# Two edits of a two-layer decoder: the order of the passes over the first layer's memory keys, and the chunk numbers at which the second layer's weight sums are made

## The chip, the cores and the metric

One Trainium2 chip, one core. The metric is the device time of one execution in microseconds (us), lower is better. The chip's engines run side by side, each through its own queue in order: TensorE (PE, matrix products; PEld is its loading of the stationary operand), VectorE (DVE), ScalarE (ACT), GpSimd (POOL) and SyncE (SP, which here only issues transfers).

## The reference, in short

A decoder trunk of two layers over 256 tokens of width 1024, in float32, with a memory of 256 rows that both layers attend to:

```
layer 0: x += short_conv_mixer(rms_norm(x)); x += mem_cross_attention(rms_norm(x), mem_n); x += swiglu(rms_norm(x))
shared keys and values (8 heads, partial rotary) from rms_norm(x), once
layer 1: x += moba_attention(rms_norm(x), shared k, v); x += mem_cross_attention(...); x += swiglu(...)
out = rms_norm(x)

short_conv_mixer: b, c, u = split(h @ w_in); (b * causal_conv3(c * u)) @ w_out
mem_cross_attention: k, v = split(mem_n @ w_kv); softmax(q k^T / 16) v, 4 heads; @ w_o
swiglu: g, u = split(h @ w_gu); (silu(g) * u) @ w_down, inner width 2816
```

There is one block of 256 keys, so layer 1's block-sparse attention is causal attention within it.

## The kernel before

**Chunks.** All weights come as 278 chunks of 128 x 1024 float32 (512 KB each), in the order in which they are used. SyncE loads them into one of 5 raw buffers. ScalarE rounds a chunk to its high part (`hi_`, a cast to fp32r), VectorE subtracts that from the raw chunk to have the low part (`lo_`). There are 10 such split pairs. Activations are split likewise. Each product is then three matmuls: high by high, high by low and low by high.

Chunks that matter here: 0 to 7 the first layer's memory keys (`memk0`), 8 to 31 the mixer's input matrices (`wc`, `wu`, `wb`), 72 to 135 layer 0's feed-forward, 160 to 167 the second layer's memory keys, 192 to 199 its memory output (`mo1`), 200 to 207 and on its feed-forward (`wr`, `wg`, `wu`, `wd`).

**Who sets the order.** A planner writes the whole program at build time. It keeps a clock for each engine with an estimated cost per instruction. Work beside the main line (norms, evictions, splits of chunks) are side jobs, which the planner asks after each matmul (`side.poll()`) whether they are due. So an edit in one loop can also change where other engines' instructions stand in their queues. Waits between engines are semaphores.

**The first layer's memory keys** (`mem_keys("memk0", ...)`, `scaled=False`). Eight column groups j of 128 in four accumulators (`acc_memk`, one bank of 2 x 256 each), over eight chunks k. Step (k, j) has three matmuls of 128 x 256: high by high and high by low (a = 0), then low by high (a = 1). For k = 0 to 3 the a = 0 matmuls of all j come first, then the low ones; for k = 4 and 5 the three stand together for each j; k = 6 and 7 are taken bank by bank, so that a bank is done early and can be evicted (`memk_u`).

While these run, side jobs prepare the mixer's input: `rows_factor` spreads the norm factor of x over the partitions by a matmul with a diagonal matrix (two pairs of `pb_x` matmuls, from `diag`), VectorE copies it (`x_rsb`) and multiplies with it (`mix_raw`, four pieces), ScalarE casts a product to its high part and VectorE subtracts for its low part (`mix`). The next products (`cu`) read `mix` and `wc`: the first one goes over k = 0 to 7 in eight matmuls of 128 x 512; its matmuls from k = 4 read the second chunk of `wc`, and those of k = 6 and 7 the last piece of `mix`.

**The weight sums.** Three pairs of feed-forward chunks (one in layer 0, two in layer 1: `jp` 4 and 8) are multiplied by seven products instead of eight, with sums of weight quarters T1 to T4 that are made in DRAM. `sum_steps(l, jp)` gives 16 steps in a fixed order, each a half: a copy issued by SyncE (L553) or an adding transfer issued by GpSimd (L551):

```
order = (("T1", "B11", False), ("T3", "B12", False), ("T1", "B12", True), ("T3", "B22", True),
         ("T2", "T1", False), ("T2", "B22", True), ("T4", "T2", False), ("T4", "B21", True))
```

A step is hung on a chunk number: `feed.hooks[n]` is run when chunk n is about to be loaded (`Feed.load_to`). `SUMS_AT` holds the first chunk and the end for each layer, between which its steps are spread evenly. Layer 0's 16 steps stand at 44 to 100. Layer 1's 32 steps stand at 128 to 217: those of `jp` 4 from 128 to 171, those of `jp` 8 from 174 to 217. The sums of `jp` 4 are first loaded from chunk 220 on, those of `jp` 8 from 250 on.

Of the kernel before, what the change touches and what calls it, by code (L numbers as in the profile page):

```python
# [21 lines left out]
KD = D // P  # L22
# [21 lines left out]
LATER = 2000  # L44
BANKWISE = 5
GROUPS = ((8,), (4, 8))
SUMS_AT = ((44, 104), (128, 220))


class Rows:  # L50
# [196 lines left out]
class Side:  # L247
# [15 lines left out]
    def step(self, item, last=0.0):  # L263
        if item[3]:
            return
        item[3] = True
        try:
            self.clock.last = last
            pause = next(item[1])
            item[0] = self.clock.last if pause is None else self.clock.now + pause  # L270
            item[4] = pause == 0
        except StopIteration:
            item[2] = True
            self.open.remove(item)
        item[3] = False
# [123 lines left out]
def yoco_kernel(  # L399
# [27 lines left out]
    def acc_tile(name):  # L427
        return ps_acc.tile([P, 512], F32, tag="acc", name=name)
# [11 lines left out]
    def held_half(name, shape=(P, 512)):  # L440
        return halves.tile(list(shape), F32, tag="half", name=name)
# [21 lines left out]
    def mm(o, l, r, start, stop, ns):  # L463
        nc.tensor.matmul(o, l, r, start=start, stop=stop)  # L464
        clock.note("pe", ns, [o], [l, r], 200)
# [69 lines left out]
    def sum_steps(l, jp):  # L535
        for name in ("T1", "T2", "T3", "T4"):
            for i in range(2):
                weight_sums[l, jp, name, i] = aside.tile([P, 2, 2 * T], F32, name=f"{name}_{l}_{jp}_{i}")

        def step(name, source, i, add):  # L540
            dst = weight_sums[l, jp, name, i]
            if source[0] == "T":
                src = weight_sums[l, jp, source, i]
            else:
                n = quarters[l, jp, source, i]
                src = chunks[n * P:(n + 1) * P].rearrange("p (a n) -> p a n", a=2)

            def run():
                clock.free["dma"] = max(clock.free["dma"], clock.now)
                if add:  # L550
                    nc.gpsimd.dma_start(dst, src, accum_op=OP.add, max_dma_last_dim=8192)  # L551
                else:
                    nc.sync.dma_start(dst, src)  # L553
                clock.note("dma", 3300 if add else 1460, [], [])

            return run

        order = (("T1", "B11", False), ("T3", "B12", False), ("T1", "B12", True), ("T3", "B22", True),
                 ("T2", "T1", False), ("T2", "B22", True), ("T4", "T2", False), ("T4", "B21", True))
        return [step(name, source, i, add) for name, source, add in order for i in range(2)]  # L560

    plan, _, quarters, ffn_steps = weight_plan()
    feed = side.feed = Feed(clock, plan, load_chunk, split_high, split_low)
# [107 lines left out]
    ones = const.tile([P, P], F32, name="ones")  # L671
# [162 lines left out]
    def mem_keys(name, mT, wait, scaled=True):  # L834
        kT = Act(side, [])
        accs = [acc_tile(f"acc_{name}_{b}") for b in range(4)]

        def bank_done(b):
            yield wait[b]
            u, j0 = kT.units[b // 2], 2 * (b % 2)  # L840
            if not scaled:
                acc = accs[b].rearrange("p (a t) -> p a t", a=2)
                scalar.copy(u[:, j0:j0 + 2, 0, :], acc)
                yield
                vector.tensor_sub(u[:, j0:j0 + 2, 1, :], acc, u[:, j0:j0 + 2, 0, :])
                return
            yield from side.hold("half")
            k_sb = held_half("k_sb", (P, 2, T))
            vector.tensor_mul(k_sb, accs[b].rearrange("p (a t) -> p a t", a=2),
                                 m_rsb[:, None, :].to_broadcast([P, 2, T]))  # L850
            yield
            scalar.copy(u[:, j0:j0 + 2, 0, :], k_sb)
            yield
            vector.tensor_sub(u[:, j0:j0 + 2, 1, :], k_sb, u[:, j0:j0 + 2, 0, :])
            side.give("half")

        def step(k, w, j, passes=((0, 0), (0, 1), (1, 0))):

            acc = accs[j // 2][:, (j % 2) * T:(j % 2 + 1) * T]
            mT.need(k)  # L860
            x = mT.parts(k)
            for a, b in passes:
                mm(acc, w[a][:, 0, j * P:(j + 1) * P], x[b], k == a == b == 0 and j % 2 == 0,
                   k == KD - 1 and a == 1 and j % 2 == 1, 0.4167 * T + 2)
                side.poll()

        for k in range(KD - 2):
            w = feed.take(f"{name}_{k}")
            if k == 0:
                for js in ((0, 1), (2, 3, 4, 5), (6, 7)):  # L870
                    for one in ((0, 0), (0, 1)):
                        for j in js:
                            step(k, w, j, (one,))
                for j in range(KD):
                    step(k, w, j, ((1, 0),))
                feed.free()
                continue
            if not scaled and k < 4:
                for ones in (((0, 0), (0, 1)), ((1, 0),)):
                    for j in range(KD):  # L880
                        step(k, w, j, ones)
                feed.free()
                continue
            for j in range(KD):
                if j == KD - 1:
                    feed.free()
                step(k, w, j)
        ws = [feed.take(f"{name}_{k}") for k in (KD - 2, KD - 1)]
        for b in range(4):
            for i in range(2):  # L890
                for j in (2 * b, 2 * b + 1):
                    step(KD - 2 + i, ws[i], j)
            if b % 2 == 0:
                kT.units.append(acts.tile([P, 4, 2, T], F32R, tag="unit", name=f"{name}_u{b // 2}"))
            kT.add_job(b % 2, b // 2, side.start(bank_done(b)))
        feed.free(2)
        return kT

    def mem_values(name, mT):
# [128 lines left out]
    feed.limit = len(plan)  # L1028
    feed.load_to(feed.lows + RAWS)
    memk0 = mem_keys("memk0", mT0, (1, 3000, 6000, 9000), False)  # L1030


# [6 lines left out]
        feed.hooks[36 + k] = [put_aside(k)]  # L1039

    for l in range(2):
        steps = [step for jp in GROUPS[l] for step in sum_steps(l, jp)]
        first, end = SUMS_AT[l]
        for n, step in enumerate(steps):
            feed.hooks.setdefault(first + (end - first) * n // len(steps), []).append(step)


    def short_conv(act, into):
# [506 lines left out]
    def moba(src, into):  # L1555
# [103 lines left out]
        proj_rows(act, "v1", keep_v)  # L1659
        mem_bank(1)  # L1660
        memk1 = mem_keys("memk1", mT1, (1, 1, 3000, 6000))
        side.finish(every)
        for job in attending.values():
# [96 lines left out]
```

## Time and profile before

| what | value |
|---|---|
| time, median of 3 runs | 784.99 us (784.41 to 785.51) |
| profiled execution: time, span | 784.93 us, 783.2 us |
| TensorE clock granted, mean | 0.998 |
| TensorE busy | 773.2 us (99%), 4147 matmuls |
| VectorE, ScalarE, GpSimd busy | 573.6, 458.9, 36.8 us |
| moved by DMA | 182.71 MB, 233 GB/s on average |

The span is the time between the first and the last recorded instruction; the execution's own time is 1.7 us longer. A line of a timeline gives start, length (us), engine, line, operation, what is written and read, and in brackets the idle time before it and what ended it. Matmuls overlap, so the distance between starts, not the length, is what one costs. Nearly all lines of ScalarE and VectorE carry L242 and those of TensorE L464, the helpers that record an operation, so lines are told apart by the names of their tiles.

### The profile page before, as it was taken

The numbers are of one execution on the slowest core, as the hardware profiler recorded it, in microseconds if no ns is written. First come the engines' busy times: TensorE is split into PE (matmuls) and PEld (weight loads), VectorE is DVE, ScalarE is ACT, GpSimd is POOL, SyncE is SP. The second block draws the span as 40 slices with busy tenths as digits, with TensorE's granted clock in tenths as the row PEclk, the third lists the DMA queues.
The fourth block names the chain that finished last, engine by engine and source line by source line (L and its number), as shares of the span: only waits on it lengthen the run. The fifth ranks groups of instructions, "written<-read, shape, count | busy, mean of one in ns | idle before, by whom it ended". The sixth has DMA issues, their size and how long they took to land.

```text
span 783.2 us, 11229 instructions
## 1 busy us (share of the span) xinstructions
PE 773.2 (99%) x4147; PEld 664.0 (85%) x4147; DVE 573.6 (73%) x872; ACT 458.9 (59%) x728; POOL 36.8 (5%) x68
## 2 busy tenths in 40 slices
PE   9999999999999999999999999999999999999996
PEld 8988888898888888888888889888988788888885
DVE  6988887768785666687766657877868776966874
ACT  6875665665654555566664573655756456655751
POOL 1000011000100000000110010030001000000000
PEclk9999999999999999999999999999999999999999
DMA  9776888916576755699787456899646746855931
GB/s 345 284 269 212 276 287 233 376 60 233 176 237 238 219 182 202 209 360 342 219 298 254 165 162 226 285 278 332 193 152 183 261 152 226 324 164 206 335 127 54
DMA packets 48807, 182.71 MB, mean 233 GB/s; under 512 B 6256, under 2 KB 7280, under 8 KB 46576
## 3 DMA queue, kind: packets, MB, share of 16 engines
q1 hardware_dynamic: 45968, 166.79, 59.5%
q0 software_dynamic: 2208, 14.68, 9.2%
q8 instruction: 32, 0.52, 0.3%
q10 hardware_dynamic: 576, 0.52, 0.2%
q14 instruction: 23, 0.19, 0.1%
HBM read 178.82 MB, written 28.31 MB: 264 GB/s over the span
## 4 chain that ended last, share of the span: by engine, by line
PE 93%; DVE 1%; DMA 1%; ACT 1%; issue 1%; POOLq 0%; DVEq 0%; ACTq 0%; SPq 0%
PE gu L464 17%; PE ff L464 14%; PE seven L464 7%; PE q_acc L464 6%; PE cu L464 6%; PE acc_mo L464 6%; PE acc_memv L464 6%; PE rows L464 4%; PE acc_memk L464 4%; PE pb L464 3%; PE acc_v L464 3%; PE acc_q L464 3%; PE acc_cout L464 3%; PE acc_o L464 3%; PE acc_k L464 3%; PE po L464 2%
## 5 line engine op out<-in xcount | busy, mean ns | idle before, releaser
L464 PE MATMUL ff<-hi_wd,guT 128*128 128x512 f32 (+1 forms) x352 | 108.3, 388 | 0.0
L464 PEld LDWEIGHTS ff<-hi_wd,guT 128*128 128x128 f32 x352 | 65.8, 188 | 12.8
L464 PE MATMUL ff<-lo_wd,guT 128*128 128x512 f32 (+1 forms) x176 | 68.3, 388 | 0.0
L242 DVE TENSOR_TENSOR gu_sb<-gu_sb,gu 128x256 f32<-128x256 f32 x48 | 20.0, 421 | 57.8 <-ACT gu_sb L242 56.9
L242 DVE TENSOR_TENSOR lo_wd<-raw_wd,hi_wd 128x1024 fp32r<-128x1024 f32 x44 | 53.5, 1221 | 7.4 <-ACT hi_wd L242 7.4
L242 ACT CAST hi_wd<-raw_wd 128x1024 fp32r<-128x1024 f32 x44 | 46.1, 1050 | 14.0 <-DMA raw_wd<-in_chunks_dram 13.0
L242 ACT COPY gu_sb<-gu 128x256 f32<-128x256 f32 x48 | 17.9, 372 | 62.1 <-PE gu L464 61.6
L464 PE MATMUL gu<-ffn,hi_wg 128*128 128x512 f32 x192 | 48.0, 390 | 0.0
L464 PE MATMUL gu<-ffn,hi_wu 128*128 128x512 f32 x192 | 47.6, 390 | 0.0
L464 PE MATMUL acc_memk<-mT,hi_memk 128*128 128x256 f32 x256 | 43.6, 287 | 0.1
L242 ACT CAST hi_wu<-raw_wu 128x1024 fp32r<-128x1024 f32 x32 | 33.5, 1051 | 15.3 <-DMA raw_wu<-in_chunks_dram 11.4
L464 PEld LDWEIGHTS gu<-ffn,hi_wg 128*128 128x128 f32 x192 | 35.9, 188 | 7.3
L464 PEld LDWEIGHTS gu<-ffn,hi_wu 128*128 128x128 f32 x192 | 35.8, 188 | 7.3
L464 PE MATMUL rows<-hi_wr,ffn 128*128 128x512 f32 x128 | 40.7, 395 | 0.0
L464 PE MATMUL acc_mo<-hi_mo,oT_mem 128*128 128x512 f32 x128 | 40.6, 393 | 0.0
L464 PE MATMUL acc_memv<-hi_memv,mT 128*128 128x512 f32 x128 | 39.6, 390 | 0.0
L242 DVE TENSOR_TENSOR lo_wu<-raw_wu,hi_wu 128x1024 fp32r<-128x1024 f32 x32 | 38.8, 1221 | 0.8 <-ACT hi_wu L242 0.5
L464 PEld LDWEIGHTS acc_memk<-mT,hi_memk 128*128 128x128 f32 x256 | 37.8, 193 | 0.8 <-ACT hi_memk L242 0.7
L464 PEld LDWEIGHTS ff<-lo_wd,guT 128*128 128x128 f32 x176 | 33.2, 188 | 6.3
L242 POOL TENSOR_TENSOR rs<-ms,neg_half 128x1 f32<-128x1 f32 x14 | 13.5, 964 | 469.1 <-DVE ms L242 459.8
L464 PE MATMUL q_acc<-mem,hi_mq 128*128 128x512 f32 x128 | 32.4, 394 | 0.0
L464 PE MATMUL acc_memk<-mT,lo_memk 128*128 128x256 f32 x128 | 31.2, 287 | 0.7 <-DVE lo_memk L242 0.5
(277 smaller groups left out, 1952.0 us busy)
## 6 DMA issues: line engine op xcount, KB each, us to landing
raw_wd<-in_chunks_dram SPq DMA_DIRECT2D x44, 512.0 KB, 5.3
raw_wu<-in_chunks_dram SPq DMA_DIRECT2D x32, 512.0 KB, 4.8
T<-in_chunks_dram POOLq DMA_DIRECT2D x24, 512.0 KB, 7.9
raw_wg<-in_chunks_dram SPq DMA_DIRECT2D x24, 512.0 KB, 5.1
raw_wT<-T SPq DMA_DIRECT2D x24, 512.0 KB, 4.9
raw_wB<-in_chunks_dram SPq DMA_DIRECT2D x18, 512.0 KB, 5.0
raw_memv<-in_chunks_dram SPq DMA_DIRECT2D x16, 512.0 KB, 5.4
raw_mq<-in_chunks_dram SPq DMA_DIRECT2D x16, 512.0 KB, 6.6
```

The costliest lines, as they stand in the source:

```text
L242: return call(out, *args, **kw)
L464: nc.tensor.matmul(o, l, r, start=start, stop=stop)
```

## The change

In `mem_keys` the unscaled case (only `memk0`) now takes chunks k = 0 to 6 with all a = 0 matmuls first and then the low ones; only k = 7 is taken bank by bank, with both column groups' a = 0 matmuls ahead of the low ones. The second layer's keys keep their order. `SUMS_AT` gets a range for each `jp`: layer 0 as before (44 to 100), layer 1's `jp` 4 at 108 to 153 and `jp` 8 at 157 to 202.

```diff
-SUMS_AT = ((44, 104), (128, 220))
+SUMS_AT = (((44, 104),), ((108, 157), (157, 206)))
...
-        for k in range(KD - 2):
+        whole = KD - 2 if scaled else KD - 1
+        for k in range(whole):
...
-            if not scaled and k < 4:
+            if not scaled:
                 for ones in (((0, 0), (0, 1)), ((1, 0),)):
                     for j in range(KD):
                         step(k, w, j, ones)
...
-        ws = [feed.take(f"{name}_{k}") for k in (KD - 2, KD - 1)]
+        ws = [feed.take(f"{name}_{k}") for k in range(whole, KD)]
         for b in range(4):
-            for i in range(2):
-                for j in (2 * b, 2 * b + 1):
-                    step(KD - 2 + i, ws[i], j)
+            for i, w in enumerate(ws):
+                for ones in (((0, 0), (0, 1), (1, 0)),) if scaled else (((0, 0), (0, 1)), ((1, 0),)):
+                    for j in (2 * b, 2 * b + 1):
+                        step(whole + i, w, j, ones)
...
-        feed.free(2)
+        feed.free(len(ws))
...
-        steps = [step for jp in GROUPS[l] for step in sum_steps(l, jp)]
-        first, end = SUMS_AT[l]
-        for n, step in enumerate(steps):
-            feed.hooks.setdefault(first + (end - first) * n // len(steps), []).append(step)
+        for jp, (first, end) in zip(GROUPS[l], SUMS_AT[l]):
+            steps = sum_steps(l, jp)
+            for n, step in enumerate(steps):
+                feed.hooks.setdefault(first + (end - first) * n // len(steps), []).append(step)
```

What this does to the queues, at three places. In the names, the numbers behind `memk0_` are the chunk k, and the last number is the tile's own. First TensorE's order around the second `pb_x` in the memory keys, before:

```order
L464 MATMUL acc_memk0_3_183<-mT0_1_109,hi_memk0_4_311 128x256 x2
L464 MATMUL acc_memk0_3_183<-mT0_1_109,lo_memk0_4_312 128x256
L464 MATMUL acc_memk0_0_180<-mT0_1_109,hi_memk0_5_342 128x256 x2
L464 MATMUL acc_memk0_0_180<-mT0_1_109,lo_memk0_5_343 128x256
L464 MATMUL acc_memk0_0_180<-mT0_1_109,hi_memk0_5_342 128x256 x2
L464 MATMUL pb_x_352<-diag_362,ones_102 128x128
L464 MATMUL acc_memk0_0_180<-mT0_1_109,lo_memk0_5_343 128x256
L464 MATMUL acc_memk0_1_181<-mT0_1_109,hi_memk0_5_342 128x256 x2
L464 MATMUL acc_memk0_1_181<-mT0_1_109,lo_memk0_5_343 128x256
```

and now:

```order
L464 MATMUL acc_memk0_3_183<-mT0_1_109,hi_memk0_5_352 128x256 x4
L464 MATMUL pb_x_366<-diag_367,ones_102 128x128
L464 MATMUL acc_memk0_0_180<-mT0_1_109,lo_memk0_5_353 128x256 x2
L464 MATMUL acc_memk0_1_181<-mT0_1_109,lo_memk0_5_353 128x256 x2
L464 MATMUL acc_memk0_2_182<-mT0_1_109,lo_memk0_5_353 128x256 x2
L464 MATMUL acc_memk0_3_183<-mT0_1_109,lo_memk0_5_353 128x256 x2
L464 MATMUL acc_memk0_0_180<-mT0_1_109,hi_memk0_6_371 128x256 x4
L464 MATMUL pb_x_366<-diag_395,ones_102 128x128
L464 MATMUL acc_memk0_1_181<-mT0_1_109,hi_memk0_6_371 128x256 x4
```

Before, the second `pb_x` stands behind the high matmuls of chunk 5's first bank and one low one; now it stands behind all of chunk 5 and the high matmuls of chunk 6's first bank.

Second, VectorE's order from right behind the copy of the norm factor (`x_rsb`) to the low parts of the mixer's first chunks (`wc`), before:

```order
L242 TENSOR_TENSOR mix0_raw_0_236<-mix0_raw_0_236,x_rsb_351 128x512
L242 TENSOR_TENSOR mix0_raw_1_238<-mix0_raw_1_238,x_rsb_351 128x512
L242 SCALAR_TENSOR_TENSOR lo_memk0_7_410<-raw_memk0_7_240,g_cols_106,hi_memk0_7_409 128x1024
L242 TENSOR_TENSOR mix0_0_278<-mix0_raw_0_236,mix0_0_278 128x2x256
L242 TENSOR_TENSOR mix0_raw_2_274<-mix0_raw_2_274,x_rsb_351 128x512
L242 TENSOR_TENSOR mix0_raw_3_276<-mix0_raw_3_276,x_rsb_351 128x512
L242 TENSOR_TENSOR mix0_0_278<-mix0_raw_1_238,mix0_0_278 128x2x256
L242 TENSOR_TENSOR memk0_u0_435<-acc_memk0_0_180,memk0_u0_435 128x2x256
L242 TENSOR_TENSOR mix0_1_279<-mix0_raw_2_274,mix0_1_279 128x2x256
L242 TENSOR_TENSOR mix0_1_279<-mix0_raw_3_276,mix0_1_279 128x2x256
L242 TENSOR_TENSOR lo_wc_0_0_462<-raw_wc_0_0_280,hi_wc_0_0_461 128x1024
L242 TENSOR_TENSOR lo_wc_0_1_475<-raw_wc_0_1_321,hi_wc_0_1_474 128x1024
```

and now:

```order
L242 TENSOR_TENSOR mix0_raw_0_236<-mix0_raw_0_236,x_rsb_365 128x512
L242 TENSOR_TENSOR mix0_raw_1_238<-mix0_raw_1_238,x_rsb_365 128x512
L242 SCALAR_TENSOR_TENSOR lo_memk0_7_412<-raw_memk0_7_240,g_cols_106,hi_memk0_7_411 128x1024
L242 TENSOR_TENSOR mix0_raw_2_274<-mix0_raw_2_274,x_rsb_365 128x512
L242 TENSOR_TENSOR mix0_0_278<-mix0_raw_0_236,mix0_0_278 128x2x256
L242 TENSOR_TENSOR mix0_raw_3_276<-mix0_raw_3_276,x_rsb_365 128x512
L242 TENSOR_TENSOR mix0_0_278<-mix0_raw_1_238,mix0_0_278 128x2x256
L242 TENSOR_TENSOR memk0_u0_454<-acc_memk0_0_180,memk0_u0_454 128x2x256
L242 TENSOR_TENSOR mix0_1_279<-mix0_raw_2_274,mix0_1_279 128x2x256
L242 TENSOR_TENSOR lo_wc_0_0_471<-raw_wc_0_0_280,hi_wc_0_0_470 128x1024
L242 TENSOR_TENSOR lo_wc_0_1_518<-raw_wc_0_1_321,hi_wc_0_1_517 128x1024
L242 TENSOR_TENSOR mix0_1_279<-mix0_raw_3_276,mix0_1_279 128x2x256
```

The low part of the last piece of `mix` (from `mix0_raw_3`) stood ahead of the two `lo_wc` subtractions and now stands behind them.

Third, GpSimd's queue from the second layer's last sums (the names end in layer, `jp` and half) to the norm factors (`rs`) of the second layer's feed-forward and of the output, before:

```order
L551 DMA T2_1_8_0_513<-in_chunks_dram 64x2048
L551 DMA T2_1_8_1_514<-in_chunks_dram 64x2048
L242 TENSOR_TENSOR rs_6030<-ms_6033,neg_half_100 128x1
L242 TENSOR_TENSOR rs_6093<-ms_6096,neg_half_100 128x1
L551 DMA T4_1_8_0_517<-in_chunks_dram 64x2048
L551 DMA T4_1_8_1_518<-in_chunks_dram 64x2048
L242 TENSOR_TENSOR rs_7627<-ms_7628,neg_half_100 128x1
L242 TENSOR_TENSOR rs_7716<-ms_7717,neg_half_100 128x1
```

and now:

```order
L551 DMA T2_1_8_0_503<-in_chunks_dram 64x2048
L551 DMA T2_1_8_1_504<-in_chunks_dram 64x2048
L551 DMA T4_1_8_0_507<-in_chunks_dram 64x2048
L551 DMA T4_1_8_1_508<-in_chunks_dram 64x2048
L242 TENSOR_TENSOR rs_6033<-ms_6036,neg_half_100 128x1
L242 TENSOR_TENSOR rs_6096<-ms_6099,neg_half_100 128x1
L242 TENSOR_TENSOR rs_7627<-ms_7628,neg_half_100 128x1
L242 TENSOR_TENSOR rs_7716<-ms_7717,neg_half_100 128x1
```

The two adds of T4 stood behind both factors of the feed-forward's norm and now stand ahead of them, right behind the adds of T2. On SyncE's queue their copies move likewise, from among the loads of `wg` and `wu` of the feed-forward to among those of `mo1`.

## Prediction

> **What bounds the kernel now.** I read the busy times first, then what TensorE waits for, then stretches of 10 us, and last the timelines of each engine around the waits.
>
> ```profile
> span 783.2 us, 11229 instructions
> PE 773.2 (99%) x4147; PEld 664.0 (85%) x4147; DVE 573.6 (73%) x872; ACT 458.9 (59%) x728; POOL 36.8 (5%) x68
> ```
>
> TensorE bounds it: it is busy for 773.2 of 783.2 us, so only 10.0 us are idle, and the change neither adds nor removes a matmul. All that it can win lies in those 10 us; all that it can lose is new idle time on TensorE. The waits of TensorE, longest first, say where they are:
>
> ```profile
> PE warm L464 <- DVE blank L763: 1.5, 1, 1.5
> PE pt_g L468 <- DVE gg L242: 1.3, 1, 1.3
> PE acc_memk L464 <- DVE lo_memk L242: 0.5, 1, 0.5
> PE acc_memk L464 <- DVE msp L242: 0.2, 1, 0.2
> ```
>
> The second lies in the last feed-forward block, the last two in the first layer's memory keys (`acc_memk`). The stretches show what else there is (time on each engine, clock, DMA share):
>
> ```profile
> 330.00:340.00 10.00, 10.00 (x46) 8.16 (x45) 8.35 (x9) 7.78 (x9) 0.00 (x0) 1.00 0.98 358
> 610.00:620.00 10.00, 8.71 (x41) 6.88 (x40) 6.48 (x9) 6.47 (x9) 0.00 (x0) 1.00 0.69 260
> 770.00:780.00 10.00, 6.90 (x48) 6.27 (x46) 7.17 (x23) 2.26 (x6) 1.46 (x2) 1.00 0.15 52
> ```
>
> The tail loses 3.10 us in this stretch alone, and neither edit touches it. The clock stays at 1.00. So the sum has two terms: the memory keys up to the gated convolution behind them, and the stretch at 612 us.
>
> **The edit of the memory keys.** TensorE's timeline:
>
> ```profile
> 1.46 2.95 PE L464 MATMUL warm<-blank 128*128 128x256 bf16 x13 [1.46 <-DVE blank L763]
> ...
> 10.88 2.08 PE L464 MATMUL acc_memk<-mT,hi_memk 128*128 128x256 f32 x16
> 12.80 1.12 PE L464 MATMUL acc_memk<-mT,lo_memk 128*128 128x256 f32 x8
> ...
> 16.64 0.40 PE L464 MATMUL acc_memk<-mT,hi_memk 128*128 128x256 f32 x2
> 17.21 0.39 PE L464 MATMUL acc_memk<-mT,lo_memk 128*128 128x256 f32 x1 [0.17 <-DVE msp L242]
> ...
> 20.76 0.38 PE L464 MATMUL pb_x<-diag,ones 128*128 128x128 f32 x2
> ...
> 24.86 0.39 PE L464 MATMUL acc_memk<-mT,lo_memk 128*128 128x256 f32 x1 [0.48 <-DVE lo_memk L242]
> ```
> ```profile
> 29.76 2.00 PE L464 MATMUL cu<-mix,hi_wc 128*128 128x512 f32 x8
> 31.60 1.98 PE L464 MATMUL cu<-mix,hi_wu 128*128 128x512 f32 x8
> ```
>
> Starts give the pitch: 16 high matmuls in 12.80 − 10.88 = 1.92, so 0.12 us each; 8 wide ones (`cu`) in 1.84, so 0.23 each. Chunks 4 to 7 took 29.76 − 16.64 = 13.12 us for 96 matmuls (11.52) and two pairs of `pb_x` (0.23 each, taking a pair to be like a wide matmul): 1.14 us are lost, and that is the most that this edit can win. It keeps chunk 4 from stopping for its low part, since 16 high matmuls (1.92 us) go first.
>
> But the edit also moves `pb_x`. The two pairs spread the norm factor of the first layer's input, which VectorE copies (`x_rsb`) before it multiplies anything of the mixer's input. The second pair stood behind four high matmuls and one low one of chunk 5 and now stands behind four high matmuls of chunk 6. From 16.64 chunk 4 takes 24 matmuls to 19.52, chunk 5's high ones last to 21.44, the first pair to 21.67, the low ones to 22.63, four of chunk 6 to 23.11. The second pair starts there, not at 20.76: 2.35 us later. VectorE's timeline of before:
>
> ```profile
> 21.80 0.42 DVE L242 COPY x_rsb<-pb_x 128x256 f32<-128x256 f32 x1
> 22.31 1.29 DVE L242 TENSOR_TENSOR mix_raw<-mix_raw,x_rsb 128x512 f32<-128x512 f32 x2
> 23.53 1.28 DVE L242 SCALAR_TENSOR_TENSOR lo_memk<-raw_memk,g_cols,hi_memk 128x1024 fp32r<-128x1024 f32 x1
> 24.72 0.68 DVE L242 TENSOR_TENSOR mix<-mix_raw,mix 128x512 fp32r<-128x512 f32 x1
> ...
> 27.73 1.28 DVE L242 TENSOR_TENSOR mix<-mix_raw,mix 128x512 fp32r<-128x512 f32 x2
> 28.93 2.36 DVE L242 TENSOR_TENSOR lo_wc<-raw_wc,hi_wc 128x1024 fp32r<-128x1024 f32 x2
> 31.20 0.68 DVE L242 TENSOR_TENSOR memk_u<-acc_memk,memk_u 128x512 fp32r<-128x512 f32 x1
> ```
>
> `x_rsb` started at 21.80, right behind the low part of chunk 6. Now it waits for the pair: 23.11 + 0.38 (that row's own length) and a semaphore's 0.1 (mix_raw at 22.31 began 0.09 behind the copy's end) is 23.6, which is 1.8 later. From there I add pitches of the rows: copy 0.51 → 24.1; two mix_raw products 1.22 → 25.3; chunk 7's low part 1.19 → 26.5; then, in the new order, mix_raw, mix, mix_raw, mix, `memk_u`, mix at 0.60 each → 30.1; two `lo_wc` 2.27 → 32.4. Only now comes the last mix part: 32.4 to 33.1. Before, it was done at 29.0, since it stood ahead of the two `lo_wc`.
>
> Who waits for it? The seventh matmul of the first `cu` product. On TensorE chunk 7's first low matmul waits for a low part that ends at 26.6 (high ones done at 26.2, so 0.4 lost), and the keys end at about 29.05, not 29.76. `cu` starts there. ScalarE, in its rows of before,
>
> ```profile
> 22.07 1.14 ACT L242 ACTIVATE hi_memk<-raw_memk,g_cols 128x1024 fp32r<-128x1024 f32 x1
> ...
> 26.22 1.14 ACT L242 CAST mix<-mix_raw 128x512 fp32r<-128x512 f32 x2
> 27.26 2.01 ACT L242 CAST hi_wc<-raw_wc 128x1024 fp32r<-128x1024 f32 x2
> ```
>
> ended the first `hi_wc` at 28.3. In the new order a mix cast stands ahead of each, and those wait for the late products: the two end at about 29.1 and 30.8. So the fifth matmul waits from 30.0 to 30.8, and the seventh from 31.3 to 33.1. Two matmuls later (0.46) the next product starts at 33.56 instead of 31.60: **+2.0 us**. Every later wait in this stretch had 0.9 us or more to spare in the order that I followed, and TensorE has no idle time behind it to take the delay up. Bounds: −1.1 (nothing late) and +2.6 (the casts and the 0.60 steps 10% longer).
>
> **The edit of the sums, at 612 us.** What the four engines and the queues did there, in time order:
>
> ```profile
> 590.52 0.56 POOL L242 TENSOR_TENSOR rs<-ms,neg_half 128x1 f32<-128x1 f32 x1 [38.44 <-DVE ms L242]
> ...
> 598.17 1.62 POOL L551 DMA_DIRECT2D T<-in_chunks_dram  x2
> ```
> ```profile
> 604.12 7.57 DMA raw_wd<-in_chunks_dram
> ```
> ```profile
> 610.56 1.05 ACT L242 CAST hi_wd<-raw_wd 128x1024 fp32r<-128x1024 f32 x1 [3.74 <-DMA raw_wd<-in_chunks_dram]
> 611.77 1.05 ACT L242 CAST hi_wd<-raw_wd 128x1024 fp32r<-128x1024 f32 x1 [0.16 <-DMA raw_wd<-in_chunks_dram]
> 612.72 0.38 ACT L242 ACTIVATE sg<-rows 128x256 f32<-128x256 f32 x1
> ```
> ```profile
> 611.94 0.39 PE L464 MATMUL rows<-hi_wr,ffn 128*128 128x512 f32 x1
> ```
> ```profile
> 613.61 0.44 PE pt_g L468 x2
> ```
> ```profile
> raw_wd<-in_chunks_dram SPq DMA_DIRECT2D x44, 512.0 KB, 5.3
> ```
>
> The last two adding transfers of the sums (T4 of pair 8) were issued at 598.17. Behind them `raw_wd` took 7.57 us against its median of 5.3. ScalarE waited 3.74 us for it, and behind its casts stood `sg`, from which `gg` and then the transpose `pt_g` come. TensorE was out of work at 611.94 + 0.23 = 612.17 and went on at 613.61: 1.44 us. In the new order these adds stand on GpSimd's queue ahead of the norm factor that ran at 590.52, so they are issued at least 13.5 us ahead of that load (604.12). With the median the last cast would end 2.3 us sooner, enough to cover 1.44: **−1.44 us**. Bounds: −1.44, and 0 if another transfer makes `raw_wd` late.
>
> **The other 31 steps.** Each of layer 1's 32 steps (half copies on SP's queue, half adds on GpSimd's) moves up by 14 to 20 chunks. On both queues they pass loads and norm factors and add no bytes. The earliest now fall into layer 0's own sum stage at 320 to 345 us, where the DMA share is already 0.98 for 10 us (above) and ScalarE's longest wait for a sum is
>
> ```profile
> 330.60 1.05 ACT L242 CAST hi_wT<-raw_wT 128x1024 fp32r<-128x1024 f32 x1 [1.76 <-DMA raw_wT<-T]
> ```
>
> TensorE is busy for all 10.00 us there, through that wait, so 1.76 us of delay is covered; what covers it are the split chunks waiting in the ten pairs. I cost these steps at 0, with +1.4 (a stop like that at 612) as the upper bound and −0.2 as the lower.
>
> **Sum.** 784.93 (the profiled execution, 0.06 below the median of 784.99; 1.7 of it lies around the span) + 2.0 − 1.44 + 0 = **785.5 us**. A measurement of this kernel can tell about 0.2% (1.6 us) from no change: the likeliest result is no change.
>
> **Rivals.** *Faster:* the factor comes late but costs nothing, since the last mix part was done 2.1 us before its matmul (29.0 against the seventh start, 29.76 + 6 × 0.23 = 31.14). Then 784.93 − 1.14 − 1.44 = 782.4. Against it: the delay of 1.8 alone would fit into 2.1, but the two `lo_wc` ahead of it take 2.27 more. It decides if the last mix part ends before 30.0. Halfway cases (net −0.4 in the keys) give 783.1 to 784.4.
>
> *Slower:* the moved transfers hold layer 0's sum stage. If the loads of T there land more than 2 to 4 us later than now, ScalarE's casts come so late that TensorE stops; priced like 612 us, at 1.4, this gives 786.9. For it: the share of 0.98; against it: no TensorE idle time for the same traffic in layer 1.
>
> *Clock:* the new pause of 1.8 us (31.3 to 33.1, with 0.8 shortly ahead of it) could cost TensorE its full clock. In the trace 1.3 us idle at 612 left the clock at 1.00. The 13 warm-up matmuls at the start took 2.95 us, 0.23 each against 0.12: such a stretch again is some +1.4, so 786.9. The Trainium skill ("TensorE: Matmul & The Clock Gate", Part 1: The HAM clock gate) has the clock halved after an idle window of about 3.4 us. By that rule a pause of 1.8 us should not do it; if it did, its window at half clock would cost an estimated 1.7 us. No run here shows a pause of that length in mid-kernel.
>
> **Chances.** Main case, 784.8 to 786.3: 0.5. Halfway: 0.12. Faster rival: 0.14. Slower rival: 0.2. Clock: 0.04. The range 782.3 to 787.1 takes in the single rivals and leaves out two stops together. Faster by over 0.2% (below 783.4) needs the keys to gain: 0.17 with the lower halfway cases; slower (above 786.6): 0.24; within: 0.59.
>
> **What would show it.** Right: `x_rsb` near 23.6; a wait of the seventh `cu` matmul on a mix part behind two `lo_wc`, second product at about 33.6; no wait of `pt_g` near 612; no new row in TensorE's waits between 320 and 400. Wrong: `cu` running through from 28.6, `raw_wd` still landing in 7 us, or waits on split chunks in layer 0's sums.

## The result, and the profile after

The changed kernel takes 792.13 us (median of 5 runs, 789.79 to 794.20) against 785.24 us (5 runs, 784.41 to 785.51): a ratio of 1.0088, with a 95% interval of 1.0067 to 1.0110. It is slower by 6.9 us, and the forecast of 785.5 us is wrong. The profiled execution has a span of 790.0 us, 6.8 more than that of before (783.2). Of all executions of the kernels below, one ran in a slower state (962.66 us at a mean granted clock of 0.752, of the new keys with pair 8 alone moved); it is in none of the ratios and counts.

TensorE's waits in the changed kernel (total us, times, longest):

```profile
PE pt_r L468 <- DVE r L242: 2.3, 1, 2.3
PE cu L464 <- DVE mix L242: 1.6, 1, 1.6
PE warm L464 <- DVE blank L763: 1.5, 1, 1.5
PE acc_memk L464 <- ACT hi_memk L242: 0.9, 1, 0.9
PE seven L464 <- DVE g L242: 0.8, 1, 0.8
PE ff L464 <- ACT guT L242: 0.7, 1, 0.7
PE gu L464 <- ACT hi_wu L242: 0.5, 1, 0.5
PE cu L464 <- ACT hi_wc L242: 0.3, 1, 0.3
PE acc_memk L464 <- DVE lo_memk L242: 0.2, 1, 0.2
```

The wait of `pt_g` is gone, the wait on `mix` is there as forecast, and four waits are new to which the forecast's sum gave no price: `seven`, `gu`, `ff` and `pt_r`. To see what each costs, I compared the times at which TensorE first uses each of the 278 chunks in the two traces. The difference moves only at these places: +0.8 at the start (the wait on `hi_memk`, before anything that differs), +2.0 at the keys, +0.3 near 55 us, +2.8 between 336 and 390 us, +2.2 ahead of the queries at 416 us, +0.1 later, −1.5 at 612 us. Before rounding these add up to 6.8.

**The keys went as forecast.** The changed kernel's TensorE and then VectorE in the first 35 us:

```profile
17.45 2.08 PE L464 MATMUL acc_memk<-mT,hi_memk 128*128 128x256 f32 x16
...
33.87 0.73 PE L464 MATMUL cu<-mix,hi_wc 128*128 128x512 f32 x2 [1.64 <-DVE mix L242]
34.44 1.99 PE L464 MATMUL cu<-mix,hi_wu 128*128 128x512 f32 x8
```
```profile
24.32 0.42 DVE L242 COPY x_rsb<-pb_x 128x256 f32<-128x256 f32 x1 [1.29 <-PE pb_x L464]
...
30.85 2.36 DVE L242 TENSOR_TENSOR lo_wc<-raw_wc,hi_wc 128x1024 fp32r<-128x1024 f32 x2
33.12 0.69 DVE L242 TENSOR_TENSOR mix<-mix_raw,mix 128x512 fp32r<-128x512 f32 x1
```

From chunk 4 to the second product it is 34.44 − 17.45 = 16.99 us, before 31.60 − 16.64 = 14.96: +2.03 for a forecast of +2.0. The norm factor is copied late, the last part of mix comes behind the two `lo_wc`, and the seventh matmul waits for it.

**So did the stop at 612 us.** The stretch that had 8.71 us of TensorE work before has no gap now:

```profile
610.00:620.00 10.00, 10.00 (x46) 8.20 (x45) 9.22 (x11) 5.78 (x8) 0.00 (x0) 1.00 0.71 228
```

ScalarE, which waited 3.74 us for the landing of `raw_wd` before, now waits for TensorE alone, and briefly:

```profile
615.40 1.05 ACT L242 CAST hi_wd<-raw_wd 128x1024 fp32r<-128x1024 f32 x1 [0.29 <-PE rows L464]
616.79 1.05 ACT L242 CAST hi_wd<-raw_wd 128x1024 fp32r<-128x1024 f32 x1 [0.33 <-PE rows L464]
```

**What the forecast missed** lies where pair 4's steps went. GpSimd's adds in the changed kernel, and the chain of waits behind them:

```profile
323.31 0.78 POOL L551 DMA_DIRECT2D T<-in_chunks_dram  x1 [11.48 <-DMA T<-in_chunks_dram]
328.07 0.78 POOL L551 DMA_DIRECT2D T<-in_chunks_dram  x1 [3.98 <-DMA T<-in_chunks_dram]
...
397.57 0.84 POOL L551 DMA_DIRECT2D T<-in_chunks_dram  x1
402.07 0.79 POOL L551 DMA_DIRECT2D T<-in_chunks_dram  x1 [3.65 <-DMA T<-T]
```
```profile
329.12 8.48 DMA raw_wT<-T
...
337.68 1.06 ACT hi_wT L242
...
338.77 0.13 DVE lo_wT L242
338.89 1.01 issue
339.91 0.70 DVE g L242
...
340.65 3.01 PE seven L464 x12
...
399.63 13.11 DMA raw_q<-in_chunks_dram
...
412.84 1.16 ACT hi_q L242
...
415.75 0.37 DVE r L242 x2
...
416.26 0.63 PE pt_r L468 x4
```

The load of a layer-0 sum that was issued at 329.12 takes 8.48 us; the same load took 4.55 before. ScalarE casts it when it lands, VectorE's subtraction `lo_wT` waits for the cast, `g` stands behind that subtraction on VectorE, and TensorE waits for `g`. At 399.63 a chunk of the queries takes 13.11 us to land while two adds run; its cast and its subtraction hold the rotation of the keys (`r`), and `pt_r` waits. In both places the work that TensorE waits for is small and has no data from the late load. It only stands behind that load's cast on ScalarE or its subtraction on VectorE.

### The profile page after: what moved, and what is told of

The parts are those of the page before. It is cut to its first block, busy times and chain, and to the rows that moved or that the text cites. A ratio compares the mean times of both kernels' runs of the same rounds, so it can differ in the third digit from the quotient of the medians.

```text
span 790.0 us, 11218 instructions
## 1 busy us (share of the span) xinstructions
PE 775.0 (98%) x4147; PEld 664.3 (84%) x4147; DVE 573.1 (73%) x872; ACT 457.9 (58%) x728; POOL 37.3 (5%) x68
## 4 chain that ended last, share of the span: by engine, by line
PE 87%; DMA 5%; DVE 3%; ACT 2%; issue 2%; SPq 0%; POOLq 0%; DVEq 0%; ACTq 0%
PE gu L464 16%; PE ff L464 13%; PE seven L464 6%; PE q_acc L464 6%; PE rows L464 6%; PE acc_mo L464 6%; PE acc_memv L464 6%; PE acc_memk L464 5%; PE cu L464 4%; PE acc_v L464 3%; PE acc_q L464 3%; PE acc_o L464 3%; PE acc_cout L464 3%; PE po L464 2%; PE s L464 2%; PE pb L464 2%
## 5 line engine op out<-in xcount | busy, mean ns | idle before, releaser
L464 PE MATMUL acc_memk<-mT,hi_memk 128*128 128x256 f32 x256 | 41.1, 288 | 0.9 <-ACT hi_memk L242 0.9
L242 DVE TENSOR_TENSOR lo_wT<-raw_wT,hi_wT 128x1024 fp32r<-128x1024 f32 x24 | 28.5, 1221 | 7.7 <-ACT hi_wT L242 7.7
L242 ACT CAST hi_wT<-raw_wT 128x1024 fp32r<-128x1024 f32 x24 | 24.7, 1054 | 14.6 <-DMA raw_wT<-T 14.3
```

What stands on the lines that cost most here:

```text
L242: return call(out, *args, **kw)
```

## Experiments

Ratios are to the kernel before on the same chip, with 95% intervals.

**The two edits and the two pairs apart.** Old keys with the new chunk numbers:

```diff
-SUMS_AT = ((44, 104), (128, 220))
+SUMS_AT = (((44, 104),), ((108, 157), (157, 206)))
```

> Only the sums' new chunk numbers; the memory keys as before. Theory: the two edits add up, and the sums alone cost what the two traces show between 330 and 420 us (+5.0) less what they show at 612 us (-1.46): +3.6, about 788.8 us. Rival: the sums only hurt because the keys' delay of 2 us shifts them against the loads; then the sums alone give -1.4, about 783.8 us.

Measured 789.08 us, ratio 1.0052 (1.0036 to 1.0068): +4.1 us or, by medians, +4.6. The sums alone do most of the harm; they need no help from the keys.

The new keys with the old chunk numbers:

> Only the new order of the first layer's memory keys; the sums as before. Theory: +2.0 to +2.3 us (the last part of mix comes behind two lo_wc), about 787.4 us, with the second product at about 33.6 to 34.4 us and the stop at 612 us still there. Rival: the delay shifts later transfers too, so the stop at 612 us or the sum stage changes by 1 us or more.

Measured 788.25 us, ratio 1.0041 (1.0029 to 1.0053), which is more than forecast. Its profiled execution was the fastest of its runs (786.42) and shows the second product 1.92 us later than before; what the slower runs have on top is taken up below.

Only pair 8 early, pair 4 as before:

```diff
+SUMS_AT = (((44, 104),), ((128, 174), (157, 206)))
```

> Only the sums of pair 8 are moved (157 to 202); those of pair 4 and the keys as before. Theory: the stop at 612 us goes and nothing else changes: -1.4 us, about 783.8 us. Rival: the earlier transfers of pair 8 hold up the loads of the second layer's keys, queries and outputs (chunks 157 to 202) as those of pair 4 do in layer 0: 0 or more, 785 us or above.

Measured 783.47 us, ratio 0.9987 (0.9979 to 0.9996). This is the best version with the old keys: faster than before by 0.4 to 2.1 permille, 11 runs within 783.21 to 783.93. TensorE's waits in it are two:

```profile
PE warm L464 <- DVE blank L763: 1.5, 1, 1.5
PE acc_memk L464 <- DVE msp L242: 0.2, 1, 0.2
```

Only pair 4 early, pair 8 as before:

```diff
+SUMS_AT = (((44, 104),), ((108, 157), (174, 220)))
```

> Only the sums of pair 4 are moved (108 to 153); those of pair 8 and the keys as before. Theory: these alone bring the waits between 330 and 420 us: +5.0 us, about 790.2 us, and the stop at 612 us stays. Rival: the loss needs both pairs, since T4 of pair 4 and the copies of pair 8 meet near 412 us: +2.8 or less, below 788.2 us.

Measured 789.21 us, ratio 1.0055 (1.0040 to 1.0069). So pair 4's 16 steps carry the loss, and pair 8's carry the gain at 612 us.

**Why pair 4's steps cost.** Either the bytes that they move, or the waits that they put into the queues. Here each of pair 4's transfers moves an eighth, in the same place. The kernel leaves out most of the sums by this, so pair 4's products use other data; eight plain copies at chunks 160 to 181 write over them:

```diff
+                if (l, jp) == (1, 4):
+                    dst_, src_ = dst[:16], src[:16]
...
+            feed.hooks.setdefault(160 + 6 * n + 3 * i, []).append(fill(name, source, i))
```

> Both pairs' sums at the new numbers, old keys, but pair 4's 16 transfers move an eighth of their bytes each, in the same places of the queues and with the same waits (the sums are then overwritten by eight plain copies at chunks 160 to 181, so pair 4's products use other data than the seven-product scheme needs). Theory: the loss between 330 and 420 us is one of bytes (landings of the chunks get longer), so nearly all of it goes: 783.5 to 784.5 us. Rival: it comes from the order in the queues (loads behind copies and adds that wait): it stays, 788 us or above.

Measured 783.67 us, ratio 0.9988 (0.9979 to 0.9997): the loss is gone with the bytes, though every wait and place in a queue stayed. A small transfer also lands sooner (medians of 3.3 to 5.2 us in this window, for 5.4 to 8.3), so the waits for it are shorter too, and this kernel alone doesn't part the two. The changed kernel's trace does in part: between 290 and 425 us none of SyncE's waits is for a copy or an add of a sum. Only one of the new waits is left, with 0.5 us:

```profile
PE gu L464 <- ACT hi_wu L242: 0.5, 1, 0.5
```

It is 0.48 us in every profile in which T1 and T3 come at 108, whatever their size, so this one comes from the order and not from the bytes.

The landings from 300 to 420 us say the same. In the changed kernel, then in this one (transfers, size each, median us to landing):

```profile
raw_wT<-T SPq DMA_DIRECT2D x8, 512.0 KB, 7.4
raw_k<-in_chunks_dram SPq DMA_DIRECT2D x8, 512.0 KB, 7.4
raw_q<-in_chunks_dram SPq DMA_DIRECT2D x8, 512.0 KB, 7.0
```
```profile
raw_wT<-T SPq DMA_DIRECT2D x8, 512.0 KB, 4.6
raw_k<-in_chunks_dram SPq DMA_DIRECT2D x8, 512.0 KB, 4.7
raw_q<-in_chunks_dram SPq DMA_DIRECT2D x8, 512.0 KB, 4.4
```

In the kernel before these medians were 4.7, 5.1 and 5.4 us, and the loads of `raw_wd` in this window had 7.4, where the changed kernel has 5.1. So there, too, some loads were late, but others, and TensorE did not stop for them.

Next, only the first eight of pair 4's steps early (T1 and T3), the last eight where they were:

```diff
+                if (l, jp) == (1, 4) and n >= 8:
+                    at = 128 + 46 * n // 16
```

> Both pairs' sums at the new numbers, old keys, but pair 4's last eight steps (T2, T4) stay where they were (151 to 171); only T1 and T3 come early. Theory: the stops in layer 0's last part (330 to 380 us, about 2 us) stay, the one ahead of the queries (410 us, 2 to 3 us) goes: about 785.7 us. Rival: T1 and T3 alone lose nothing, since there are half as many transfers in 20 chunks: 783.5 us.

Measured 784.46 us, ratio 1.0003 (0.9994 to 1.0011). Against pair 8 alone (0.9987) T1 and T3 cost about 1.2 us, and T2 and T4 the larger rest, 3.8 us by the ratios (1.0052 with all sums early against 1.0003). My split of 2 and 2 to 3 was off, and the runs suggest why: the stops of 336 to 380 us seem to differ from execution to execution. The profiled one, the slowest of its 11 runs (786.55), shows 0.9, 0.6 and 0.5 us there; the others were not profiled, but at a median of 784.46 they should lose less.

Then pair 4 halfway, from chunk 118 on:

```diff
+SUMS_AT = (((44, 104),), ((118, 166), (157, 206)))
```

> Both pairs' sums early, old keys, but pair 4 from chunk 118 to 163 (halfway). Theory: the loss is set by what meets the loads of layer 0's own sums (chunks 114 to 125), which are issued before chunk 118's hook runs in full: 1 to 3 us of loss, 784.5 to 786.5 us. Rival: as with 108, since the adds still meet the last chunks of layer 0: 788 us or above.

Measured 787.75 us, ratio 1.0047 (1.0031 to 1.0063). My expectation fails: the loss hardly shrinks. In its trace, of the slowest of its six runs (791.70), the stops have moved (1.4 us on `u`, 0.6 on a `lo_wB`, 0.6 on a `lo_wd` and 2.2 on `r`). Between 108 and the old 128 no other place was tried.

**Why the keys cost more than 2.0.** The following kernels all have pair 8 alone moved, so that neither 612 us nor pair 4 disturbs. First the new keys as they are:

> The changed order of the memory keys with the sums of pair 8 alone moved. Theory: the two effects add up: +2.0 for the keys (last part of mix behind two lo_wc, behind a late norm factor) and -1.4 at 612 us, about 785.5 us; second product at 33.5 us from the start of an undisturbed beginning. Rival: moving the keys by 2 us also costs later, as the keys' own run of 788.3 may suggest: 787 us or more.

Measured 787.39 us, ratio 1.0037 (1.0024 to 1.0051): 3.9 us above the old keys with the same sums (783.47), where 2.0 was expected. Some 0.6 of the missing 1.9 us may lie in the old keys: from chunk 4 to the second product they take 14.95 us in the profile of before, but 14.34 (17.05 to 31.39) in that of pair 8 alone. Then the convolution asked for all of mix before it takes weights:

```diff
                 if name not in taken:
+                    if jp == 0 and name == "wc":
+                        for k in range(KD):
+                            act.need(k)
```

> As the kernel with the changed keys and pair 8 moved, but the convolution asks for all of mix before it takes its first weight chunks, so the last part of mix stands ahead of the two lo_wc again; the norm factor stays late. Theory: that takes away 1.8 of the 2.0 us (the second product starts at about 31.8 us, held by ScalarE's second hi_wc): about 783.7 us. Rival: the late norm factor alone is the cost, and the place of mix behind lo_wc is not: 785.5 us as without it.

Measured 786.24 us, ratio 1.0025 (1.0016 to 1.0034): of the expected 1.8 us only about 1.1 came back. The wait on mix is gone and the second product starts at 31.98 us, but new waits took its place near 50 us, on casts of later chunks; why these are late was not followed further (the waits of this kernel, largest two behind the start):

```profile
PE pb L464 <- ACT hi_wb L242: 0.8, 1, 0.8
PE cu L464 <- ACT hi_wu L242: 0.5, 2, 0.2
```

Then the norm factor early, with the last part of mix left behind the two `lo_wc`:

```diff
-            if not scaled:
+            if not scaled and k != 5:
```

> As the kernel with the changed keys and pair 8 moved, but chunk 5 goes column by column as before, which puts both pb_x pairs into its first half (norm factor at about 21 us); the last part of mix stays behind the two lo_wc. Theory: the seventh product matmul waits to about 31.7 us, second product at 32.2: +0.6 against the old keys, about 784.1 us. Rival: with the factor early the order behind it costs nothing: 783 us or below.

Measured 785.02 us, ratio 1.0011 (1.0002 to 1.0020). Its second product starts at 32.35 us for an expected 32.2, but its chunk 4 started early, at 16.18; from there it is 16.17 us, 1.2 more than before where 0.6 was expected. The factor's place (with the form of chunk 5 that sets it) is worth 2.4 us in the medians (787.39 − 785.02), of which its profile shows 0.8 in the keys (16.17 against 16.98 us with the new keys). The mean clocks of the runs, taken up below, suggest where a part of the rest is. Then both mends:

> Both mends of the keys together, with pair 8 alone moved. Theory: the keys end about 1 us sooner than in the old order, but ScalarE's second hi_wc (about 30.6 us) becomes the limit, so the second product starts at 31.1 to 31.6 us: 0 to -0.5 against the old keys, about 783.2 us. Rival: the whole 1.1 us that the keys lost before is won: about 782.4 us.

Measured 784.48 us, ratio 0.9998 (0.9989 to 1.0007): not better than the old keys with these sums, by medians 1.0 us worse. The first product starts at 29.40, earlier than before, but the second lasts 2.41 us instead of 1.98, and about 0.6 us more goes near the start of the next one, where a wait of 0.2 us on `conv` shows. The 1.1 us that the keys lose in the old order was not won in any form that I tried.

For the missing part I took the new keys' profile again:

> The changed keys with pair 8 alone moved, once more, for a profile. The median of this kernel lies 3.9 us above that of the old keys with the same sums, of which the late last part of mix explains 2.0. Theory: the rest is a second stop behind it in the convolution, where ScalarE's casts of the next chunks now come late (1 to 2 us between 40 and 70 us). Rival: the rest is lost at the start, ahead of chunk 4, where runs differ by up to 0.9 us in any kernel.

Measured 787.31 us, ratio 1.0026 (1.0015 to 1.0036); the profiled execution took 787.78. Its wait on mix is 1.64 us as in the other profiles, and no second wait follows. But the second product, eight matmuls, lasts 3.40 us instead of 2.0 (TensorE, then the clock in the last column but two):

```profile
33.83 0.73 PE L464 MATMUL cu<-mix,hi_wc 128*128 128x512 f32 x2 [1.64 <-DVE mix L242]
34.40 3.40 PE L464 MATMUL cu<-mix,hi_wu 128*128 128x512 f32 x8
```
```profile
32.00:34.00 2.00, 0.36 (x2) 0.17 (x2) 2.00 (x4) 2.00 (x3) 0.00 (x0) 1.00 0.39 129
34.00:36.00 2.00, 2.00 (x7) 1.59 (x8) 2.00 (x3) 1.22 (x2) 0.00 (x0) 0.66 0.72 208
36.00:38.00 2.00, 2.00 (x6) 1.56 (x5) 2.00 (x3) 0.89 (x1) 0.00 (x0) 0.50 0.90 286
```

The granted clock fell to half for about 3.4 us right behind the stop, and TensorE lost 1.6 us by it (against the old keys the first use of each chunk is 3.0 us late ahead of it and 4.6 behind it). Neither of my two expectations said that. To test it, seven matmuls on zeros fill the stop, and nothing else changes:

```diff
+            if part == 0 and k == 6 and fill:
+                for _ in range(fill.pop()):
+                    nc.tensor.matmul(acc.rearrange("p r t -> p (r t)").rearrange("p (a b) -> p a b", a=4), zeros, zeros[:, None, :].to_broadcast([P, 4, P]), start=False, stop=False)
```

> The changed keys with pair 8 alone moved, and seven matmuls on a tile of zeros (1.6 us) added to the first cu product ahead of its seventh matmul, so that TensorE works through the stop while the last part of mix is as late as before; nothing else is changed. Theory: the rest of the loss is the clock, which falls to half behind the stop in most executions; with the stop filled it stays, so the time falls from 787.3 to about 785.5 us and the runs lie within 1 us of each other. Rival: the rest is lost elsewhere and the seven matmuls win nothing: 787.3 us.

Measured 786.34 us, ratio 1.0021 (1.0012 to 1.0030), 11 runs from 785.52 to 786.89. TensorE works through the stop, mix is as late as before, and the second product has its full clock:

```profile
31.40 1.68 PE L585 MATMUL cu<-zeros 128*128 128x512 bf16 x7
33.20 0.74 PE L464 MATMUL cu<-mix,hi_wc 128*128 128x512 f32 x2
33.78 2.02 PE L464 MATMUL cu<-mix,hi_wu 128*128 128x512 f32 x8
```

By medians that wins 1.0 us, half of what was missing: without the filling 9 of 12 runs were at 786.86 or above, with it one of 11. The intervals of the two ratios overlap, so the size is not settled. The mean granted clock, on record for each run, agrees: profiles with a stretch at half clock in mid-kernel have a mean of 0.995 or 0.996, those without 0.997 to 0.999. Without the filling 7 of the 12 runs are at 0.995 or 0.996, and they take 787.32 to 787.78 us; the other five take 785.28 to 787.12. With it none of the 11 is below 0.997, and none is in the kernel with the early factor, though that one has a stop of 1.66 us.

A part of the rest shows in this profile: a stop of 0.68 us at 54.02 us, where `pb_rs` waits for VectorE, together with chunk use slipping by 0.9 there. Other profiles of the new keys show it at 0.0 to 0.3 us. How often it comes is open.

## Why the prediction was wrong

- **Bound, right.** TensorE stayed the limit. In the profiled execution the loss lies at stops of TensorE, and the granted clock stood at 1.00 through them; in three of the five runs (792.13 to 794.20) the mean clock of 0.993 to 0.996 suggests that some was lost to the clock as well.
- **Keys, +2.0, right in the profile.** +2.03 by the very chain: second `pb_x`, `x_rsb` (23.6 forecast; 24.32 − 0.81 for the later start = 23.5), mix behind two `lo_wc`, seventh matmul. The whole cost is larger, 3.2 us by the ratio of the keys alone. The clock behind the stop of 1.6 us is about 1 us of it by the filled stop; the remainder is not located.
- **Sums at 612 us, −1.44, right.** −1.46 in the profile; pair 8 alone measured about −1.0 by the ratio.
- **The other steps, 0, wrong.** This is the step that failed. I saw that the earliest steps would fall into 320 to 345 us, with the DMA share at 0.98, and still priced them at 0, with 1.4 as the upper end. They cost 4.3 to 5.1 us (pair 4 alone +4.3 by its ratio, +4.7 by medians; all sums early, 1.0052, against pair 8 alone, 0.9987, +5.1). In place of no cost the runs show that their bytes delay the loads beside them, and that a late load holds small work in the queues of ScalarE and VectorE for which TensorE then stops. I took "TensorE idles nowhere here" for cover and priced one stop, where the 16 transfers over some 100 us make three, and the new order a fourth (`gu`). I looked only at layer 0's sum stage; by the run with T1 and T3 alone the larger part comes with T2 and T4 further on, between 360 and 412 us. (Two slips in that term: 32 steps less the two adds at 612 us are 30, and they move by 15 to 20 chunks.)
- **The cover that I named, the split chunks, did shrink, but that alone is not the cost.** The first chunk `wg` behind layer 0's sums had its high part at 343.38 us and was used at 355.02 before (11.6 us early), and at 357.54 and 359.26 after (1.7). The load is not to blame: it landed at 349.33. ScalarE's order is:

```profile
356.00 0.59 ACT L242 CAST guT<-pt_g 128x512 fp32r<-128x512 f32 x1 [6.45 <-PE pt_g L468]
356.49 2.00 ACT L242 CAST hi_wg<-raw_wg 128x1024 fp32r<-128x1024 f32 x2
```

  The cast of `guT`, which waits for TensorE, now stands ahead of `hi_wg`. With pair 4's bytes cut to an eighth the lead is 1.7 us as well, and only the 0.5 us of `gu` is lost. With pair 4 from 118 on it is 6.6 us, and the loss is nearly the whole. Whether the bytes would cost as much with the old lead was not tested.
- **Slower rival, right in kind** (the moved transfers hold ScalarE's casts, and TensorE stops behind them), with a chance of 0.2 and a price more than three times too small.
- **Clock rival, wrong in its chance.** I gave it 0.04 by one row, 1.3 us idle at 612 us with the clock at 1.00. At stops of 1.6 to 2.7 us the clock did fall in four profiles (the keys again, all sums early, pair 4 alone, pair 4 from 118 on). The cost, 1.4, was about right (1.6), but not by its row: the granted clock stands at 1.00 through the warm-up matmuls that it was taken from. The rule of the Trainium skill that I set beside it ("TensorE: Matmul & The Clock Gate", Part 1: The HAM clock gate), an idle window of about 3.4 us, doesn't fit the trace here: 0.27 and 1.64 us of idle time with two matmuls between them were enough. The length of the half-clock stretch, about 3.4 us, does agree with the window that the page names.

The range, 782.3 to 787.1, did not reach the result, because it took in only one such stop.

## What to carry to other kernels

Transfers with slack of their own are not free to move: price them by the landings of the loads that they will run beside; that the bounding engine doesn't idle there now says little. In these in-order queues a late load held everything behind its cast and its subtraction, so look at what small work stands behind each. And since stops of 1.6 to 2.7 us brought a stretch at half clock in some executions here, such a stop is worth a second term for the clock, with a chance.

## What was not expected of the hardware

The clock of TensorE fell to half at short stops, and not each time. The stop of 2.3 us at 416 us in the changed kernel left it at 1.00; the same stop of 2.67 us with the sums alone did not, nor did one of 1.83 us with pair 4 alone (the stop on `pt_g`, which ends at 618.89 us there). The rows of the stretches, in that order, with the clock in the last column but two:

```profile
410.00:420.00 10.00, 7.70 (x39) 6.16 (x38) 5.15 (x12) 5.38 (x7) 0.00 (x0) 1.00 0.85 342
```
```profile
410.00:420.00 10.00, 7.79 (x33) 6.56 (x34) 6.67 (x13) 5.85 (x7) 0.00 (x0) 0.83 0.51 184
```
```profile
620.00:630.00 10.00, 10.00 (x40) 8.04 (x40) 6.78 (x11) 4.77 (x7) 0.00 (x0) 0.85 0.65 201
```

The one profile of the kernel before shows no fall behind its stop of 1.3 us. Of the 87 runs of that kernel with a clock on record, two are at 0.996, and they are its slowest, 787.09 and 787.10 us; so it may have happened there too, rarely. That the same stop brings a fall in one execution and not in another explains a part of the scatter, as far as the mean clocks go. It isn't the whole: the kernel with the early factor (a stop of 1.66 us, 784.54 to 786.69) and the one with T1 and T3 alone early (783.57 to 786.55) scatter by 2 to 3 us with no run below 0.997, while pair 8 alone stays within 0.7 us. What decides whether a stop brings a fall is open; only the filled stop tested it.
